# Every product of a two-layer encoder in plain float32 instead of three float32r products

## The chip, the cores and the metric

One core of a Trainium2 chip runs the whole program. The metric is device time of one execution in microseconds, the median of several runs. TensorE (PE in the profile) does the matrix products, VectorE (DVE) and ScalarE (ACT) the elementwise work, and the SyncE queue (SP) issues all transfers.

## What is computed

A trunk of two layers over 1024 tokens of width 1024. All inputs are float32. Cut to what matters:

```python
for layer in range(2):
    hn = rmsnorm(h, norm1_g[layer])
    proj = hn @ w_in[layer]                      # 1024 x 3328: u, q, k, v, gate_a, gate_b
    y_a = s5_branch(u, ...)                      # state-space branch, two directions, then GLU (512 x 512)
    y_b = windowed_gqa(q, k, v, sink, bias)      # 8 query heads of 64, 2 key heads, window 128
    merged = gate_a * (y_a @ w_branch_a[layer]) + gate_b * (y_b @ w_branch_b[layer])
    h = h + merged @ w_out[layer]
    hn2 = rmsnorm(h, norm2_g[layer])
    ff = silu(hn2 @ ffn_w_gate[layer]) * (hn2 @ ffn_w_up[layer])     # width 2816
    h = h + ff @ ffn_w_down[layer]
return rmsnorm(h, final_g)
```

## The kernel before, in words

Activations lie with channels on the 128 partitions and tokens along the free axis, in tiles of 128 x 512 (two token halves, `h` = 0 and 1). A dense layer is a loop over output tiles; for each, `chain` runs over the tiles of the contraction and adds into one 128 x 512 PSUM tile. A weight "granule" is 128 x 1024 floats, eight weight tiles that serve one output tile (or two) for both token halves, so 16 products.

**Two parts for every operand.** Each operand of a dense product is kept as a pair: `hi` is the value rounded to float32r (a ScalarE copy), `lo` is the rest (a VectorE subtraction). `split` (lines 87 to 91) does it for activations, `parts` (97 to 105) for weights, and `chain` (107 to 118) forms every product as three matmuls:

```python
mm(ps, lhsT=wh, rhs=xh, start=k == 0, stop=False)          # line 116
mm(ps, lhsT=wh, rhs=xl, start=False, stop=False)           # line 117
mm(ps, lhsT=wl, rhs=xh, start=False, stop=k == n - 1)      # line 118
```

The names in the trace: `pj` input projections, `glu`, `br` the two branch products, `wo` the output projection, `fg`, `fu`, `dn` the feed-forward's gate, up and down products.

**Attention.** A head has 64 channels, half of the partitions. For the scores (`att_scores`, line 716, tile `s`) the query tile holds hi of a head on one half of the partitions and lo on the other; the key tile holds the same keys on both halves, once as hi and once as lo, so that two matmuls over all 128 partitions give the whole product. For p times v (`att_values`, line 756, tile `pv`) the value tile holds hi and lo in two column halves; the sum of both halves is made on ScalarE and VectorE (lines 758 and 768). The probabilities are turned with transposes on TensorE (line 744, tile `pt`).

**The state-space branch** was in plain float32 all along: `s5x` (line 865, outputs on alternate halves of 64 PSUM partitions), `s5y` (lines 907 to 910), `psE` (lines 565 and 569, outputs on four quarters), and also the bias table `psb` (line 196, one 512-column product).

**What sets the order.** The program is a list of items (`build`), mixed by hand so that state-space and softmax work on VectorE lies beside dense products; `emit` runs through it. Weights are loaded on the SP queue into two `raw` buffers (`fetch`), then split into one of three hi/lo pairs, `LOOK` = 2 granules ahead. TensorE, VectorE and ScalarE run their items in the order of the list in the first part of layer 0 (`self.strict`).

Of the kernel before, what the change touches and what calls it, by code (L numbers as in the profile page):

```python
# [9 lines left out]
F32R = mybir.dt.float32r  # L10
# [29 lines left out]
LOOK = 2  # L40
# [3 lines left out]
W_BUFS = 3  # L44
# [4 lines left out]
class Granule:  # L49


    def __init__(self, src, n, slots=False):
        self.src, self.n, self.slots = src, n, slots
        self.raw = self.hi = self.lo = None
# [18 lines left out]
class Trunk:  # L73
# [13 lines left out]
    def split(self, src, name):  # L87
        hi, lo = self.A(name + "h", F32R), self.A(name + "l", F32R)
        self.nc.scalar.copy(hi, src)
        self.nc.vector.tensor_tensor(lo, src, hi.bitcast(F32), SUB)  # L90
        return hi, lo

    def fetch(self, g):
        g.raw = self.pw.tile([P, DM], F32, tag="raw", name="raw", bufs=2)
        self.nc.sync.dma_start(g.raw[:, :g.n], g.src)

    def parts(self, g):
        nc, n = self.nc, g.n
        if g.slots:
            g.hi, g.lo = self.A("whs", F32R), self.A("wls", F32R)  # L100
        else:
            g.hi = self.pw.tile([P, DM], F32R, tag="whi", name="whi", bufs=W_BUFS)
            g.lo = self.pw.tile([P, DM], F32R, tag="wlo", name="wlo", bufs=W_BUFS)
# [19 lines left out]
    def emit(self):  # L123
# [8 lines left out]
        self.order, self.fetched, self.split_ = order, 0, 0  # L132
        pos = {id(g): i for i, g in enumerate(order)}
        strict = None
        for i, (fn, gs) in enumerate(self.seq):
# [7 lines left out]
            if gs:  # L143
                self.ahead(max(pos[id(g)] for g in gs) + 1)
                held = [g.src.tensor.name for g in order[:self.split_] if last[id(g)] >= i and not g.slots]
                assert len(held) <= W_BUFS, (i, held)
            fn()
            if gs:
                n = max(pos[id(g)] for g in gs) + 1
                while self.split_ < len(order) and self.split_ < n + (7 if order[self.split_].slots else LOOK):  # L150
                    held = sum(last[id(g)] > i and not g.slots for g in order[:self.split_])
                    if held >= W_BUFS and not order[self.split_].slots:
                        break
                    self.ahead(self.split_ + 1)
                    if order[self.split_ - 1].slots:
                        break
# [5 lines left out]

    def ahead(self, n):
        n = min(n, len(self.order))
        while self.split_ < n:
            self.fetch_to(min(self.split_ + 2, len(self.order)))
            self.parts(self.order[self.split_])
            self.split_ += 1
# [86 lines left out]
    def normed(self, x, h, gi, name, out):  # L255

        nc = self.nc
        ys = {}
        for m in range(KT + 1):
            if m < KT:  # L260
                ys[m] = self.A("y")
                nc.vector.scalar_tensor_tensor(ys[m], x(m), self.gains[:, gi, m:m + 1], self.r[h], MUL, MUL)
            if m:
                out[m - 1] = self.split(ys.pop(m - 1), name)
            if m in (2, 4, 6):
                yield
# [10 lines left out]
    def first_pair(self, h, m, x):  # L277

        nc, g = self.nc, self.gains[:, 0, m:m + 1]
        hi, lo = self.A("xgh", F32R), self.A("xgl", F32R)  # L280
        nc.scalar.activation(hi, x, AF.Copy, scale=g)
        nc.vector.scalar_tensor_tensor(lo, x, g, hi.bitcast(F32), MUL, SUB)
        self.xg[h][m] = (hi, lo)
# [344 lines left out]
    def key_tiles(self, kn, kv, T):  # L628

        nc = self.nc  # L630
        s = slice(64 * kv, 64 * kv + 64)
        hh, ll = self.A(f"kh{kv}{T}", F32R), self.A(f"kl{kv}{T}", F32R)
        for o in (slice(0, 64), slice(64, 128)):
            nc.scalar.copy(hh[o], kn[T][s])
        for o in (slice(0, 64), slice(64, 128)):
            nc.vector.tensor_tensor(ll[o], kn[T][s], hh[s].bitcast(F32), SUB)
        self.kt[kv, T] = (hh, ll)

    def value_tiles(self, vn):
        nc = self.nc  # L640
        for T in range(2):
# [3 lines left out]
            for b in range(2):  # L645
                vt = self.A("vt", F32R)
                o = vt.rearrange("p (k s d) -> p k s d", s=2, d=64)
                src = pt[:, b * 256:(b + 1) * 256].rearrange("p (k d) -> p k d", d=64)
                nc.scalar.copy(o[:, :, 0], src)
                nc.vector.tensor_tensor(o[:, :, 1], src, o[:, :, 0].bitcast(F32), SUB)  # L650
                self.vt.append(vt)

    def tile_q(self, l, i, xs=None):
        nc = self.nc
        st = {}

        def done(h, ps):
# [6 lines left out]
            lo, up = slice(0, 64), slice(64, 128)  # L664
            for T in range(2):
                e, o = self.A(f"qe{i}{T}", F32R), self.A(f"qo{i}{T}", F32R)
                nc.scalar.copy(e[lo], qn[T][lo])
                nc.vector.tensor_tensor(e[up], qn[T][lo], e[lo].bitcast(F32), SUB)
                nc.scalar.copy(o[up], qn[T][up])
                nc.vector.tensor_tensor(o[lo], qn[T][up], o[up].bitcast(F32), SUB)  # L670
                self.qt[2 * i, T], self.qt[2 * i + 1, T] = e, o
# [22 lines left out]
    def att_scores(self, l, kv, b):  # L694
# [8 lines left out]
        for h in range(4):  # L703
            hd = 4 * kv + h
            q = self.qt[hd, Tq][:, (3 - oq) * P:(4 - oq) * P]
            ps = self.PS("s")
            spans = []
            a = k0
            while a < k1:
                e = min(k1, (a // 4 + 1) * 4)  # L710
                spans.append((a, e))
                a = e
            for w in range(2):
                for a, e in spans:
                    kk = self.kt[kv, a // 4][w]
                    nc.tensor.matmul(ps[:, (a - k0) * P:(e - k0) * P], lhsT=q, rhs=kk[:, (a % 4) * P:(a % 4 + e - a) * P],
                                     start=w == 0 and a == k0, stop=w == 1 and e == k1)
            x = self.A("x")
            V.tensor_tensor_reduce(out=x[:, :n], in0=ps[:, :n], in1=self.bias[hd][:, bo:bo + n], op0=ADD, op1=ALU.min,  # L719
                                   scale=-1.0, scalar=self.nsink[:, l, hd:hd + 1], accum_out=nm[:, h:h + 1])  # L720
            ex.append(x)
# [16 lines left out]
    def att_transpose(self, ex, k0, k1):  # L738
        nc = self.nc
        out = []  # L740
        for k in range(k1 - k0):
# [3 lines left out]
            out.append(self.split(ps, "p"))  # L745
        return out

    def att_values(self, kv, b, pt, k0, k1):
# [3 lines left out]
        for k in range(n):  # L752
            vb = k0 + k
            v = self.vt[vb // 2][:, (vb % 2 * 2 + kv) * P:(vb % 2 * 2 + kv + 1) * P]
            for w in range(2):
# [7 lines left out]
        w = slice((3 - o) * P, (4 - o) * P)  # L763
        for h in range(4):
            y = self.yb[2 * kv + h // 2, T]
            hp = slice(64 * (h % 2), 64 * (h % 2) + 64)
            c = slice(h * P, (h + 1) * P)
            nc.vector.tensor_tensor(y[hp, w], ps[0:64, c], t[0:64, c], ADD)

    def att_pairs(self, kv):  # L770

        nc = self.nc
        for i in range(2):
            kt = 2 * kv + i
            for h in range(2):
                hi, lo = self.A(f"ybh{kt}", F32R), self.A(f"ybl{kt}", F32R)
                for T in range(2):
                    s = self.yb[kt, T][:, ::-1].rearrange("p (n j) -> p j n", j=8)[:, 4 * h:4 * h + 4]
                    w = slice(64 * T, 64 * T + 64)
                    ho = hi.rearrange("p (j n) -> p j n", j=4)[:, :, w]  # L780
                    lw = lo.rearrange("p (j n) -> p j n", j=4)[:, :, w]
                    nc.scalar.copy(ho, s)
                    nc.vector.tensor_tensor(lw, s, ho.bitcast(F32), SUB)
                self.ybp[h][kt] = (hi, lo)
# [225 lines left out]
    def glu_items(self, l):  # L1010
        nc, V = self.nc, self.nc.vector
        gs = [self.pair_weights("w_glu", l, i) for i in range(2)]
        z, zp = {}, [[None] * 4, [None] * 4]
# [8 lines left out]
        def pairs(k):  # L1022
            for h in range(2):
                zp[h][k] = self.split(z[k, h], f"zp{k}")

        def run(h, m):
            ps = self.PS("glu")
            self.chain(ps, gs[m // 2], (m % 2) * HC, zp[h])
            t = self.A("gt")
# [145 lines left out]
    def build(self):  # L1175
# [14 lines left out]
        def start():  # L1190
# [9 lines left out]
            for h in range(2):  # L1200
                self.ahead(h + 1)
                for m in range(KT):
                    self.first_pair(h, m, xs[h][m])
# [232 lines left out]
```

## Time and profile before

| | before |
|---|---|
| median of 3 runs | 2757.1 us (2756.61 to 2757.65) |
| the profiled execution's own time | 2755.04 us |
| its span, first to last instruction | 2753.3 us |
| TensorE matmul busy | 2687.4 us, 13122 records |
| VectorE busy | 1548.3 us, 3321 records |
| ScalarE busy | 877.1 us, 1637 records |
| mean granted TensorE clock | 0.988 of full |

How to read it: a matmul's record runs from its start to the end of its results, so neighbours overlap. What a matmul costs in a dense stretch is the distance from one start to the next (or a stretch divided by its number of records), not the record's length. A float32r matmul has one record. A plain float32 matmul of the program has two records of equal form: the loop around line 907 runs 64 times (2 layers, 8 calls, 2 x 2 inside) and the trace has 128 records of it.

### The profile page before, as it was taken

The page shows a single profiled execution, that of the slowest core. Times are in us where ns is not written, and L with a number is a line of the kernel's source. Part 1 is how long each engine was busy: PE and PEld are TensorE (multiplying, and loading weights), DVE is VectorE, ACT ScalarE, POOL GpSimd, SP SyncE. Part 2 cuts the span into 40 slices and gives each one's busy share as a digit, 9 for nine tenths or more (in the row PEclk, how much of TensorE's full clock was granted, in tenths as well). Part 3 has the DMA queues.
Part 4 walks back from the last instruction along what each step waited for, and adds up shares of the span by engine and source line. Part 5 has one row for each costly group of instructions (what it writes and reads, how often), then busy time and mean ns, then how long its engine had stood idle before and what let it go on. Part 6 is the DMA issues. An engine that isn't in the chain of part 4 may idle for free.

```text
span 2753.3 us, 33872 instructions
## 1 busy us (share of the span) xinstructions
PE 2687.4 (98%) x13122; PEld 2226.9 (81%) x13122; DVE 1548.3 (56%) x3321; ACT 877.1 (32%) x1637; POOL 0.2 (0%) x4
## 2 busy tenths in 40 slices
PE   8999988999999999999999999999999999999997
PEld 6788876787888888888888888888878888888886
DVE  9987978675744444553376877565362323232335
ACT  5336744422312222221245643353131111111112
POOL 0000000000000000000000000000000000000000
PEclk9999998999999999999999999999999999999999
DMA  3453245342122221322221236444211111111111
GB/s 118 136 182 101 90 156 163 121 167 96 44 72 68 61 77 58 94 60 90 62 92 66 66 110 200 154 142 136 90 58 34 59 45 55 39 61 35 58 50 65
DMA packets 135920, 249.91 MB, mean 91 GB/s; under 512 B 14624, under 2 KB 50720, under 8 KB 135760
## 3 DMA queue, kind: packets, MB, share of 16 engines
q1 hardware_dynamic: 135760, 247.76, 27.9%
q8 instruction: 103, 1.69, 0.3%
q14 instruction: 57, 0.47, 0.1%
HBM read 187.98 MB, written 59.72 MB: 90 GB/s over the span
## 4 chain that ended last, share of the span: by engine, by line
PE 87%; DVE 8%; ACT 2%; DMA 1%; issue 1%; SPq 1%; DVEq 0%; ACTq 0%
PE fu L116 6%; PE fu L118 6%; PE fu L117 6%; PE dn L116 6%; PE fg L116 6%; PE fg L118 6%; PE dn L118 6%; PE dn L117 6%; PE fg L117 6%; PE pj L116 6%; PE pj L117 5%; PE pj L118 5%; PE wo L116 2%; PE wo L118 2%; PE wo L117 2%; PE br L117 2%
## 5 line engine op out<-in xcount | busy, mean ns | idle before, releaser
L104 ACT CAST whi<-raw 128x1024 fp32r<-128x1024 f32 (+2 forms) x240 | 228.3, 952 | 840.4 <-PE dn L117 315.5
L105 DVE TENSOR_TENSOR wlo<-raw,whi 128x1024 fp32r<-128x1024 f32 (+2 forms) x240 | 263.6, 1098 | 284.3 <-ACT whi L104 276.0
L116 PE MATMUL pj<-rah,whi 128*128 128x512 f32 x768 | 307.6, 402 | 6.8 <-DVE sm L719 6.8
L117 PE MATMUL pj<-ral,whi 128*128 128x512 f32 x768 | 302.0, 393 | 0.1
L118 PE MATMUL pj<-rah,wlo 128*128 128x512 f32 x768 | 301.7, 393 | 0.0
L117 PE MATMUL fg<-rfl,whi 128*128 128x512 f32 x704 | 274.8, 390 | 2.1 <-DVE rfl L90 2.1
L116 PE MATMUL fg<-rfh,whi 128*128 128x512 f32 x704 | 274.7, 390 | 0.0
L116 PE MATMUL fu<-rfh,whi 128*128 128x512 f32 x704 | 274.6, 390 | 0.0
L118 PE MATMUL fg<-rfh,wlo 128*128 128x512 f32 x704 | 274.0, 389 | 0.0
L117 PE MATMUL fu<-rfl,whi 128*128 128x512 f32 x704 | 274.0, 389 | 0.0
L118 PE MATMUL fu<-rfh,wlo 128*128 128x512 f32 x704 | 273.9, 389 | 0.0
L1124 DVE TENSOR_TENSOR h<-h,dn 128x512 f32<-128x512 f32 x160 | 109.7, 686 | 232.8 <-PE dn L118 232.4
L1116 DVE SCALAR_TENSOR_TENSOR ts<-fu,ts 128x512 f32<-128x512 f32 x88 | 60.8, 691 | 231.7 <-PE fu L118 231.7
L116 PEld LDWEIGHTS pj<-rah,whi 128*128 128x128 f32 x768 | 145.9, 190 | 41.3 <-DVE sm L719 8.0
L118 PEld LDWEIGHTS pj<-rah,wlo 128*128 128x128 f32 x768 | 145.5, 189 | 31.5
L117 PEld LDWEIGHTS pj<-ral,whi 128*128 128x128 f32 x768 | 145.9, 190 | 29.8 <-DVE ral L90 1.2
L117 PEld LDWEIGHTS fg<-rfl,whi 128*128 128x128 f32 x704 | 132.2, 188 | 32.6 <-DVE rfl L90 5.6
L118 PEld LDWEIGHTS fu<-rfh,wlo 128*128 128x128 f32 x704 | 132.2, 188 | 27.4
L117 PEld LDWEIGHTS fu<-rfl,whi 128*128 128x128 f32 x704 | 132.2, 188 | 27.3
L116 PEld LDWEIGHTS fg<-rfh,whi 128*128 128x128 f32 x704 | 132.2, 188 | 27.3
L116 PEld LDWEIGHTS fu<-rfh,whi 128*128 128x128 f32 x704 | 132.2, 188 | 27.2
L118 PEld LDWEIGHTS fg<-rfh,wlo 128*128 128x128 f32 x704 | 132.2, 188 | 27.2
(363 smaller groups left out, 4953.5 us busy)
## 6 DMA issues: line engine op xcount, KB each, us to landing
raw<-in_w_in SPq DMA_DIRECT2D x52, 512.0 KB
raw<-in_w_gate SPq DMA_DIRECT2D x44, 512.0 KB
raw<-in_w_up SPq DMA_DIRECT2D x44, 512.0 KB
g<-th SPq DMA_DIRECT2D x64, 256.0 KB
thr<-g SPq DMA_DIRECT2D x64, 256.0 KB
raw<-in_w_down SPq DMA_DIRECT2D x48, 256.0 KB
raw<-in_w_down SPq DMA_DIRECT2D x32, 320.0 KB
sp<-CA SPq DMA_DIRECT2D x64, 128.0 KB
```

The lines of the kernel that those rows point to most:

```text
L104: nc.scalar.copy(g.hi[:, :n], g.raw[:, :n])
L105: nc.vector.tensor_tensor(g.lo[:, :n], g.raw[:, :n], g.hi[:, :n].bitcast(F32), SUB)
L116: mm(ps, lhsT=wh, rhs=xh, start=k == 0, stop=False)
L117: mm(ps, lhsT=wh, rhs=xl, start=False, stop=False)
L118: mm(ps, lhsT=wl, rhs=xh, start=False, stop=k == n - 1)
L1116: V.scalar_tensor_tensor(s, st[h, "u"], 0.5, s, MUL, MUL)
L1124: V.tensor_tensor(x, x, ps, ADD)
```

## The change

All pairs go. Activations are single float32 tiles; weights are loaded straight into one of eight buffers (`W_BUFS` = 8, `LOOK` = 5 granules ahead) and used from there, so nothing on ScalarE or VectorE stands between the load and the product, and TensorE itself sets a weight buffer free. `chain` issues one plain float32 matmul where it issued three. Scores: keys of one head group stand twice, on both partition halves; a query tile holds two heads, one per half, and each head's product contracts over its own 64 partitions, two heads in turn, into two PSUM tiles. p times v: two heads' results go to PSUM partitions 0 to 63 and two to 64 to 127, 256 columns each, so the adding of halves after it goes too. A few factors of 0.25 and 0.5 move into other operations.

```diff
-LOOK = 2
+LOOK = 5
-W_BUFS = 3
+W_BUFS = 8
...
     def fetch(self, g):
-        g.raw = self.pw.tile([P, DM], F32, tag="raw", name="raw", bufs=2)
-        self.nc.sync.dma_start(g.raw[:, :g.n], g.src)
-
-    def parts(self, g):
...
-        nc.scalar.copy(g.hi[:, :n], g.raw[:, :n])
-        nc.vector.tensor_tensor(g.lo[:, :n], g.raw[:, :n], g.hi[:, :n].bitcast(F32), SUB)
+        g.w = self.A("ws") if g.slots else self.pw.tile([P, DM], F32, tag="w", name="w", bufs=W_BUFS)
+        self.nc.sync.dma_start(g.w[:, :g.n], g.src)
...
-        for k, (xh, xl) in enumerate(xs):
+        for k, x in enumerate(xs):
             if part is not None and k * 2 // n != part:
                 continue
             s = off + k * P
-            wh, wl = g.hi[:, s:s + P], g.lo[:, s:s + P]
-            mm = self.nc.tensor.matmul
-            mm(ps, lhsT=wh, rhs=xh, start=k == 0, stop=False)
-            mm(ps, lhsT=wh, rhs=xl, start=False, stop=False)
-            mm(ps, lhsT=wl, rhs=xh, start=False, stop=k == n - 1)
+            self.nc.tensor.matmul(ps, lhsT=g.w[:, s:s + P], rhs=x, start=k == 0, stop=k == n - 1)
...
+        for i in range(2):
+
+            pss = [self.PS("s") for _ in range(2)]
+            q = self.qt[2 * kv + i, Tq]
+            for a, e in spans:
+                for j, ps in enumerate(pss):
+                    r = slice(64 * j, 64 * j + 64)
+                    nc.tensor.matmul(ps[:, (a - k0) * P:(e - k0) * P], lhsT=q[r, (3 - oq) * P:(4 - oq) * P],
+                                     rhs=self.kt[kv, a // 4][r, (a % 4) * P:(a % 4 + e - a) * P], start=a == k0, stop=e == k1)
...
-            v = self.vt[vb // 2][:, (vb % 2 * 2 + kv) * P:(vb % 2 * 2 + kv + 1) * P]
-            for w in range(2):
-                nc.tensor.matmul(ps, lhsT=v, rhs=pt[k][w], start=k == 0 and w == 0, stop=k == n - 1 and w == 1)
-        t = self.A("pvl")
-        nc.scalar.copy(t[0:64], ps[64:128])
+            v = self.vt[vb // 4][:, vb % 4 * P + 64 * kv:vb % 4 * P + 64 * kv + 64]
+            p = pt[k].rearrange("p (i j q) -> p j i q", i=2, j=2)
+            for j in range(2):
+
+                nc.tensor.matmul(ps[64 * j:64 * j + 64, 0:256].rearrange("p (i q) -> p i q", i=2), lhsT=v, rhs=p[:, j],
+                                 start=k == 0, stop=k == n - 1)
...
-        for h in range(4):
-            y = self.yb[2 * kv + h // 2, T]
-            hp = slice(64 * (h % 2), 64 * (h % 2) + 64)
-            c = slice(h * P, (h + 1) * P)
-            nc.vector.tensor_tensor(y[hp, w], ps[0:64, c], t[0:64, c], ADD)
+        for i in range(2):
+            nc.vector.tensor_copy(self.yb[2 * kv + i, T][:, (3 - o) * P:(4 - o) * P], ps[:, i * P:(i + 1) * P])
```

How the instructions stand, at two places. First TensorE at the first down products of layer 0 (`fu` the last up product, `dn` down, `ts` the activation that was split into `ff..h` and `ff..l`). Before:

```order
L118 MATMUL fu<-rfh,wlo 128x512
L116 MATMUL dn<-ff0h,whi 128x512
L117 MATMUL dn<-ff0l,whi 128x512
L118 MATMUL dn<-ff0h,wlo 128x512
L116 MATMUL dn<-ff1h,whi 128x512
L117 MATMUL dn<-ff1l,whi 128x512
L118 MATMUL dn<-ff1h,wlo 128x512
```

Now, from the feed-forward's first products on:

```order
L97 MATMUL fg<-rf,w 128x512 x16
L97 MATMUL fu<-rf,w 128x512 x8
L97 MATMUL fg<-rf,w 128x512 x8
L97 MATMUL fu<-rf,w 128x512 x16
L97 MATMUL fg<-rf,w 128x512 x16
L97 MATMUL fu<-rf,w 128x512 x16
```

One instruction stands where three stood, with the same columns; the order of the products is as it was. Over the program 10560 such instructions become 3520.

Second, TensorE at one step of attention in layer 0 (`qe`, `qo` the query tiles with hi and lo, `kh`, `kl` the keys; now `qn` holds two heads and `kk` the keys). Before:

```order
L716 MATMUL s<-kh_2177,qe_714 128x384
L716 MATMUL s<-kl_2178,qe_714 128x384
L716 MATMUL s<-kh_2177,qo_715 128x384
L716 MATMUL s<-kl_2178,qo_715 128x384
L716 MATMUL s<-kh_2177,qe_832 128x384
L716 MATMUL s<-kl_2178,qe_832 128x384
L716 MATMUL s<-kh_2177,qo_833 128x384
L716 MATMUL s<-kl_2178,qo_833 128x384
L744 MATMUL pt<-cst,x 128x128 x8
```

Now (with the p times v of the step that follows):

```order
L658 MATMUL s<-kk_1513,qn_501 128x384 x2
L658 MATMUL s<-kk_1513,qn_537 128x384 x2
L689 MATMUL pt<-cst,x 128x128 x8
L97 MATMUL pj_1820<-ra,w 128x512 x8
L658 MATMUL s<-kk_1513,qn_501 128x384 x2
L658 MATMUL s<-kk_1513,qn_537 128x384 x2
L704 MATMUL pv<-p,vt 64x256 x4
```

Eight float32r instructions for a step's scores become four plain ones, in pairs of two heads on the two partition halves; p times v keeps its number of instructions (176 in the program), each of half the columns and half the output partitions.

## Rows read from the trace of the kernel before

**Rows 1.** The page: busy time by engine, and TensorE's busy tenths in 40 slices
```profile
PE 2687.4 (98%) x13122; PEld 2226.9 (81%) x13122; DVE 1548.3 (56%) x3321; ACT 877.1 (32%) x1637; POOL 0.2 (0%) x4
...
PE   8999988999999999999999999999999999999997
```

**Rows 2.** The page: the chain that ended last, by engine
```profile
PE 87%; DVE 8%; ACT 2%; DMA 1%; issue 1%; SPq 1%; DVEq 0%; ACTq 0%
```

**Rows 3.** Waits of PE, longest first: us in total, times, longest
```profile
PE s5x L865 <- DMA s5uk<-ud: 14.5, 4, 5.9
PE pj L116 <- ACT xgh L281: 7.1, 1, 7.1
...
PE br L116 <- ACT ybh L782: 3.8, 1, 3.8
```

**Rows 4.** Stretches of 100 us: busy us and (records) of each engine, clock, DMA
```profile
2100.00:2200.00 100.00, 100.00 (x443) 82.84 (x442) 30.03 (x41) 14.91 (x21) 0.00 (x0) 1.00 0.17 52
2500.00:2600.00 100.00, 100.00 (x443) 82.80 (x442) 32.73 (x46) 16.55 (x24) 0.00 (x0) 1.00 0.14 42
```

**Rows 5.** The same view over the whole span, line 116 alone
```profile
0.00:2754.00 2754.00, 1388.88 (x3520) 666.22 (x3520) 0.99 0.28 91
```

**Rows 6.** Line 196: durations min/median/max ns, first and last start; then the timeline
```profile
L196 PE MATMUL psb<-oh,rb x2: 584/584/585, 109.9 to 110.4; 32*8 32x512 f32 x2
...
109.92 1.01 PE L196 MATMUL psb<-oh,rb 32*8 32x512 f32 x2 [1.87 <-DMA rb<-in_rel_bias]
```

**Rows 7.** Timeline of PE: start us, us; first and last of 12 `s5y` products
```profile
404.49 0.38 PE L907 MATMUL s5y<-s5uk 128*128 128x128 f32 x2
...
406.94 0.39 PE L910 MATMUL s5y<-s5sg,s5ca 128*128 128x127 f32 x2
```

**Rows 8.** The chain in order of time: one step of scores, one of p times v
```profile
278.65 1.41 PE s L716 x8
280.06 1.39 PE pv L756 x6
```

**Rows 9.** Timeline of PE: 16 records of `s5x`, on alternate halves of the output partitions
```profile
358.19 1.10 PE L865 MATMUL s5x<-s5uk,s5wbt 128*64 128x128 f32 x16
```

**Rows 10.** The page: the splits of the weights on ACT and DVE
```profile
L104 ACT CAST whi<-raw 128x1024 fp32r<-128x1024 f32 (+2 forms) x240 | 228.3, 952 | 840.4 <-PE dn L117 315.5
L105 DVE TENSOR_TENSOR wlo<-raw,whi 128x1024 fp32r<-128x1024 f32 (+2 forms) x240 | 263.6, 1098 | 284.3 <-ACT whi L104 276.0
```

**Rows 11.** The chain in order of time: a weight load, and PE's last piece
```profile
15.11 4.29 DMA raw<-in_w_in
...
2742.08 2.09 PE psn L249 x8
```

**Rows 12.** Span and mean granted clock
```profile
core 0: 2753.3 us, clock 0.988
```

**Rows 13.** Timeline of PE after a wait of 3 us: longer records, then normal ones
```profile
454.27 1.97 PE L865 MATMUL s5x<-s5uk,s5wbt 128*64 128x128 f32 x16 [3.01 <-DMA s5uk<-ud]
...
456.77 0.63 PE L117 MATMUL br<-ybl,whi 128*128 128x512 f32 x1
457.19 0.63 PE L118 MATMUL br<-ybh,wlo 128*128 128x512 f32 x1
...
460.43 0.40 PE L117 MATMUL br<-ybl,whi 128*128 128x512 f32 x1
460.66 0.40 PE L118 MATMUL br<-ybh,wlo 128*128 128x512 f32 x1
```

**Rows 14.** Timeline of PE: six microseconds of plain float32 work, and what follows
```profile
481.89 0.38 PE L907 MATMUL s5y<-s5uk 128*128 128x128 f32 x2
...
486.84 1.10 PE L865 MATMUL s5x<-s5uk,s5wbt 128*64 128x128 f32 x16 [1.08 <-DMA s5uk<-ud]
...
488.21 0.40 PE L117 MATMUL br<-ybl,whi 128*128 128x512 f32 x1
488.45 0.40 PE L118 MATMUL br<-ybh,wlo 128*128 128x512 f32 x1
```

More of the change, by code (lines that the diff above doesn't have):

```diff
@@ L9 @@
 F32 = mybir.dt.float32
-F32R = mybir.dt.float32r
 I32 = mybir.dt.int32
@@ L53, in __init__ @@
         self.src, self.n, self.slots = src, n, slots
-        self.raw = self.hi = self.lo = None
+        self.w = None
 class Later:
@@ L143, in emit @@
             if gs:
-                self.ahead(max(pos[id(g)] for g in gs) + 1)
-                held = [g.src.tensor.name for g in order[:self.split_] if last[id(g)] >= i and not g.slots]
-                assert len(held) <= W_BUFS, (i, held)
+                n = max(pos[id(g)] for g in gs) + 1
+                self.fetch_to(n)
+                held = [g for g in order[:self.fetched] if last[id(g)] >= i and not g.slots]
+                assert len(held) <= W_BUFS, (i, len(held))
             fn()
             if gs:
[L149 to L152, printed above, removed]
+                while self.fetched < len(order) and self.fetched < n + LOOK:
+                    g = order[self.fetched]
+                    if not g.slots and sum(last[id(x)] > i and not x.slots for x in order[:self.fetched]) >= W_BUFS:
                         break
-                    self.ahead(self.split_ + 1)
-                    if order[self.split_ - 1].slots:
+                    self.fetch_to(self.fetched + 1)
+                    if g.slots:
                         break
@@ L161, in fetch_to @@
             self.fetched += 1
[L163 to L168, printed above, removed]
     def constants(self):
@@ L255, in normed @@
     def normed(self, x, h, gi, name, out):
[L257 to L265, printed above, removed]
+        for m in range(KT):
+            out[m] = self.A(name)
+            self.nc.vector.scalar_tensor_tensor(out[m], x(m), self.gains[:, gi, m:m + 1], self.r[h], MUL, MUL)
+            if m in (1, 3, 5):
                 yield
@@ L275, in first_half, with first_gain @@
         return xs
[L277 to L283, printed above, removed]
+    def first_gain(self, h, m, x):
+        self.xg[h][m] = self.A("xg")
+        self.nc.scalar.activation(self.xg[h][m], x, AF.Copy, scale=self.gains[:, 0, m:m + 1])
     def s5_scalars(self):
@@ L628, in key_tiles @@
     def key_tiles(self, kn, kv, T):
-        nc = self.nc
-        s = slice(64 * kv, 64 * kv + 64)
-        hh, ll = self.A(f"kh{kv}{T}", F32R), self.A(f"kl{kv}{T}", F32R)
+        kk = self.kt[kv, T] = self.A(f"kk{kv}{T}")
         for o in (slice(0, 64), slice(64, 128)):
[L634 to L637, printed above, removed]
+            self.nc.scalar.copy(kk[o], kn[T][64 * kv:64 * kv + 64])
     def value_tiles(self, vn):
@@ L644, in value_tiles @@
                 nc.tensor.transpose(pt[:, b * P:(b + 1) * P], vn[T][:, b * P:(b + 1) * P], self.ident)
[L645 to L651, printed above, removed]
+            self.vt.append(self.A("vt"))
+            nc.scalar.copy(self.vt[T], pt)
     def tile_q(self, l, i, xs=None):
-        nc = self.nc
         st = {}
@@ L702, in att_scores @@
         ex = []
-        for h in range(4):
[L704 to L712, printed above, removed]
-            for w in range(2):
[L714 to L721, printed above, removed]
+        spans = [(a, min(k1, (a // 4 + 1) * 4)) for a in range(k0, k1) if a == k0 or a % 4 == 0]
+        for i in range(2):
[6 more added lines that the diff above has]
+                                     rhs=self.kt[kv, a // 4][r, (a % 4) * P:(a % 4 + e - a) * P], start=a == k0, stop=e == k1)
+            for j, ps in enumerate(pss):
+                h = 2 * i + j
+                hd = 4 * kv + h
+                x = self.A("x")
+                V.tensor_tensor_reduce(out=x[:, :n], in0=ps[:, :n], in1=self.bias[hd][:, bo:bo + n], op0=ADD, op1=ALU.min,
+                                       scale=-1.0, scalar=self.nsink[:, l, hd:hd + 1], accum_out=nm[:, h:h + 1])
+                ex.append(x)
         for h in range(4):
@@ L744, in att_transpose @@
                 nc.tensor.transpose(ps[:, h * P:(h + 1) * P], ex[h][:, k * P:(k + 1) * P], self.ident)
-            out.append(self.split(ps, "p"))
+            out.append(self.A("p"))
+            nc.scalar.copy(out[k], ps)
         return out
@@ L775, in att_pairs @@
             for h in range(2):
-                hi, lo = self.A(f"ybh{kt}", F32R), self.A(f"ybl{kt}", F32R)
+                y = self.ybp[h][kt] = self.A(f"yp{kt}")
                 for T in range(2):
                     s = self.yb[kt, T][:, ::-1].rearrange("p (n j) -> p j n", j=8)[:, 4 * h:4 * h + 4]
[L779 to L784, printed above, removed]
+                    nc.scalar.copy(y.rearrange("p (j n) -> p j n", j=4)[:, :, 64 * T:64 * T + 64], s)
     def bias_load(self, kv):
@@ L1020, in prep @@
                 nc.sync.dma_start(z[k, h].rearrange("p (j n) -> p j n", j=4), self.zd[k][:, 4 * h:4 * h + 4, :])
-        def pairs(k):
-            for h in range(2):
-                zp[h][k] = self.split(z[k, h], f"zp{k}")
         def run(h, m):
             ps = self.PS("glu")
-            self.chain(ps, gs[m // 2], (m % 2) * HC, zp[h])
-            t = self.A("gt")
+            self.chain(ps, gs[m // 2], (m % 2) * HC, [z[k, h] for k in range(4)])
+            t = self.ya[h][m] = self.A(f"ya{m}")
             nc.scalar.activation(t, ps, AF.Tanh, scale=0.25)
             V.scalar_tensor_tensor(t, t, 1.0, z[m, h], ADD, MUL)
-            hi, lo = self.A(f"yah{m}", F32R), self.A(f"yal{m}", F32R)
-            nc.scalar.activation(hi, t, AF.Copy, scale=0.25)
-            V.scalar_tensor_tensor(lo, t, 0.25, hi.bitcast(F32), MUL, SUB)
-            self.ya[h][m] = (hi, lo)
         for h in range(2):
@@ L1039, in glu_items @@
                 out.append((lambda h=h, m=m: run(h, m), gs[m // 2]))
-        early = [(lambda k=k: prep(k),) for k in range(4)]
-        split = [(lambda k=k: pairs(k),) for k in range(4)]
-        return early, split, out
+        return [(lambda k=k: prep(k),) for k in range(4)], out
     def w_out_items(self, l):
@@ L1116, in up_out @@
             V.scalar_tensor_tensor(s, st[h, "u"], 0.5, s, MUL, MUL)
-            ff[h][f] = self.split(s, f"ff{f % 6}")
+            ff[h][f] = s
         def down(gi, m, h, g):
@@ L1200, in start @@
             for h in range(2):
-                self.ahead(h + 1)
                 for m in range(KT):
-                    self.first_pair(h, m, xs[h][m])
+                    self.first_gain(h, m, xs[h][m])
         self.item(start)
@@ L1274, in done_a @@
                 V.scalar_tensor_tensor(t, t, 1.0, ps, ADD, MUL)
-                V.tensor_tensor(t, t, b, ADD)
-                hi, lo = self.A(f"mgh{m}", F32R), self.A(f"mgl{m}", F32R)
-                nc.scalar.activation(hi, t, AF.Copy, scale=0.5)
-                V.scalar_tensor_tensor(lo, t, 0.5, hi.bitcast(F32), MUL, SUB)
-                self.mg[h][m] = (hi, lo)
+                mg = self.mg[h][m] = self.A(f"mg{m}")
+                V.tensor_tensor(mg, t, b, ADD)
             bb = self.branch_items(l, "w_br_b", lambda h: self.ybp[h], (), done_b)
             ba = self.branch_items(l, "w_br_a", lambda h: self.ya[h], (ta, tb), done_a)
-            early, split, glu = self.glu_items(l)
+            early, glu = self.glu_items(l)
             if l == 0:
@@ L1288, in build @@
             n = min(4, len(left))
-            self.add(early[:3] + split[:3] + left[:n // 2] + early[3:] + (pairs[:1] if l else []) + left[n // 2:n] + split[3:] +
+            self.add(early[:3] + left[:n // 2] + early[3:] + (pairs[:1] if l else []) + left[n // 2:n] +
                      (self.mix(glu, pairs[1:]) if l else glu))
```

30 lines of the change are left out of this document (5 added, 25 removed).

## The prediction, made before the changed kernel was run

> **What bounds the kernel now.** I read the page first, then the waits, then TensorE's timeline. The busy line [rows 1] has TensorE at 2687.4 us of a span of 2753.3, VectorE at 1548.3 and ScalarE at 877.1; the slices show TensorE at 9 tenths nearly everywhere. The chain that ended last is TensorE for 87% [rows 2]. The waits [rows 3] are short: the longest class is 14.5 us in all. So the kernel's time is the time of TensorE's instruction stream, and the question is what one product costs as three float32r matmuls, and what as one plain matmul.
>
> Busy time can't answer that, because records overlap. Two stretches of the feed-forward that hold nothing but chains have 443 records in 100 us each, at a granted clock of 1.00 [rows 4]: 100 / 443 = 0.2257 us from start to start. Three of them are **0.677 us per product**. Line 116 has 3520 records [rows 5], one per product, so chains take 3520 x 0.677 = 2383 us of the span.
>
> **What a plain product costs.** The kernel already runs some, each seen as two records. The only one with 512 columns is the bias table's [rows 6]: two records of 0.584 us, 1.01 us together, so the second starts 1.01 - 0.584 = 0.43 us after the first. That is nearly twice the 0.2257 us of a float32r record of the same columns, and there are two of them. The `s5y` products have 128 columns [rows 7]: from the first start to the twelfth, 2.45 us, so 2.45 / 11 = 0.2227 us per product, 0.1114 per record. Both fit two periods of the full 2.4 GHz clock per column (0.833 ns, so 0.427 us at 512 columns and 0.1067 at 128) plus about 5 ns a record. I take 2 x (0.4267 + 0.0047) = **0.863 us per product**. The lower bound is 0.853, with nothing between records; the upper one 4 x 0.2227 = 0.891, if what lies between records grows with the columns. I take the value near the lower end because the 512-column row is the nearest in form, and its 0.43 has no room for the upper one.
>
> The Trainium skill, "FP8 and Floating Point Precision", section "TensorE Precision Notes", says that a true FP32 product takes four passes through the array. Four passes at the float32r record's 0.2257 us would be 0.903 us per product and the sum below some 140 us higher; the trace shows two records per product, each about twice as long, and 0.43 us each is 0.86.
>
> **The change part by part.** All counts are of the whole program.
>
> 1. *Chains.* 3520 x (0.863 - 0.677) = **+655 us**, all of it on the path, since nothing else is longer than TensorE. By the bounds +619 and +753.
>
> 2. *Scores.* A step with three key blocks took 1.41 us for eight matmuls [rows 8]; 24 of 32 steps have that width, the other 8 two thirds of it: 24 x 1.41 + 8 x 0.95 = 41 us. Now four plain products of 384 columns, two records each of 384 x 0.833 + 5 = 325 ns: 2.60 us in a row, or 1.30 if the two partition halves run side by side. For column halves the trace shows that they do: 16 records of `s5x`, 128 columns, take 1.10 us with the last one's 0.27 [rows 9], so 0.83 / 15 = 0.055 us each, half of the 0.1114 that a lone one costs. No row has two row halves. I take side by side: 24 x 1.30 + 8 x 0.87 = 38 us, **-3 us**; the other end is +35.
>
> 3. *p times v.* 88 key blocks at 1.39 / 3 = 0.463 us [rows 8] are 41 us. Now each block has two column halves of 256 columns, two records each: 4 x 218 ns, halved by running side by side as `s5x` does: 0.436 us, 38 us, **-3 us**. One after the other it would be +36.
>
> 4. *Splits.* The weights' splits alone, 228.3 us on ScalarE and 263.6 on VectorE [rows 10], and those of activations and probabilities go. They lay beside TensorE's work and were not what it waited for, so they are worth nothing by themselves. The transposes, the state-space products and the softmax stay.
>
> 5. *Weights straight from the load.* A granule now feeds 16 x 0.863 = 13.8 us of work (10.8 before), and a load was seen to land 4.29 us after issue even in the crowded start [rows 11]. With five granules ahead I cost it at nothing. The new wait is that a load needs TensorE to be done with the buffer, and what is behind it on the SP queue (state-space loads and stores) waits too. Eight buffers and five ahead mean that the buffer asked for was left some three granules, 40 us, earlier, so I expect no queueing; if that cover is gone, the state-space loads come late and the 14.5 us of rows 3 would perhaps double, +15.
>
> 6. *Idle time and slow stretches.* TensorE is idle 2753.3 - 2687.4 = 66 us. The first 7.1 us are the load of the first operands [rows 3], and after its last piece, at 2742.08 + 2.09, come 9 us of final scaling [rows 11]; both stay. Of the other 50 (state-space loads, softmax, the split of `ybh`) I take half away: each dense item between two such steps is now 27% longer, and ScalarE and VectorE have less ahead of them. **-25 us**. The mean granted clock is 0.988 [rows 12], that is 33 us of full-speed work not done, a part of it in the idle ends. After a wait of 3 us the records run at the lower level, 1.2 GHz, for some 6 us [rows 13]: starts 0.42 us apart, and 0.23 after it. Fewer waits mean fewer such stretches: **-10 us**. Bounds for both together: 0 and -75.
>
> Sum: 2753.3 + 655 - 3 - 3 - 25 - 10 = 3367 us of span. The median of the runs is 3.8 us above the profiled span, so **3371 us**, 22% slower.
>
> **The rivals.**
>
> *The price between records is higher* (chance 0.12). At 0.891 per product, part 1 is +753 and the time 3469; at four float32r passes, 0.903, it is +796 and 3512. For it: no row shows a long run of 512-column plain products. Against it: the 0.43 us of rows 6.
>
> *The halves don't run side by side* (0.07). Scores alone: 3371 + 38 = 3409; p times v too: 3448. For it: no row with row halves, and two heads are issued in turn, each with two records. Against it: rows 9, for column halves.
>
> *The two records of a product lie over each other, or one of them is spared* (0.04): this ends on the other side. One record for a product costs 0.431 us instead of 0.677, the chains 1519 us instead of 2383, and the kernel some 2757 - 864 - 6 = 1887 us, with TensorE still the longest engine after the splits are gone. The mechanism would be that the 128-column products are paced by the loading of their weights, so that their 0.1114 us says nothing of the columns, and that the bias product, with 8 output columns, is a case apart. It decides from a price below 0.677 + 0.012 = 0.689 us per product, where the sum of the parts crosses zero. Against it: rows 6 have both a load of 8 weight columns and 0.43 us from record to record. The Trainium skill, "Perfetto Trace Analysis", section "Engine Utilization", gives the array half its output rate for FP32_LOW_HIGH; read as a price of a whole product, that would be this rival. Each record here does run at half the rate, but there are two.
>
> *Plain work does not hold the full clock* (0.02). At 1.2 GHz throughout, 3520 products would cost 1.73 us each and the kernel over 6400 us. Against it: 6 us of nothing but plain work with one 1.08 us wait in it [rows 14], after which float32r starts are 0.24 us apart, the pace of the full clock.
>
> **How the numbers follow.** My forecast has 0.74. Its own range: chains at 0.853 with most idle time gone give 3371 - 36 - 40 = 3295, at 0.875 with none gone 3371 + 42 + 35 = 3448; I don't expect both ends at once. The range of 8 in 10, 3320 to 3480, holds most of the forecast, the rival of the halves whole and the lower end of the rival of the price (3469). Left out are 3512, the fast rival and the slow clock. Slower by over 0.2% (what a measurement of this kernel can tell from no change): 0.74 + 0.12 + 0.07 + 0.02 = 0.95. Faster: 0.04. The remaining 0.01 is for prices that happen to meet at the crossing.
>
> **What would show it.** In the changed kernel's profile, a stretch of 100 us in the feed-forward should hold 100 / 0.4314 = 232 matmul records, 116 products, at clock 1.00. 215 to 225 records mean the higher price; 443 would mean that a plain record costs what a float32r one did. The records of line 97 should number 7040. A step of scores should take about 1.3 us from its first start to the next work, 2.6 if the halves run one after the other; a step of p times v 1.3 against 2.6. TensorE should be busy 98 to 99% of the span, VectorE well under half. The prediction is wrong if the feed-forward's pace is not 0.43 us a record, or if TensorE waits for weights.

## The result, and the profile after

The changed kernel takes 3336.98 us (median of 4 runs, 3335.31 to 3337.30) against 2757.38 us before (2756.61 to 2759.78): ratio 1.2099, 95% interval 1.2078 to 1.2120. It is 21% slower; 3371 us within 3320 to 3480 was forecast. The profiled execution took 3337.3 us with a span of 3335.5, so the span grew by 582.2 us.

The page of the changed kernel, as in [rows 1, 2]: busy time, TensorE's slices, its granted clock, and the chain that ended last.

```profile
PE 3294.5 (99%) x9778; PEld 1538.9 (46%) x9778; DVE 1019.8 (31%) x2593; ACT 483.5 (14%) x1097; POOL 0.2 (0%) x4
...
PE   8999998999999999999999999999999999999998
...
PEclk9999999999999999999999999999999999999999
...
PE 97%; DVE 2%; DMA 1%; ACT 0%; SPq 0%; issue 0%; DVEq 0%; ACTq 0%
```

TensorE was the bound before and is it more purely now: its share of the chain rose from 87 to 97%, while VectorE lost 528 us of work and ScalarE 394. None of that work comes back as time. TensorE's busy time grew by 607.1 us and its idle time fell from 65.9 to 41.1, which makes the 582.2.

The dense products of the changed kernel: the costliest group on TensorE, then all records of line 97 over the span and a stretch of the feed-forward as in [rows 4, 5].

```profile
L97 PE MATMUL pj<-ra,w 128*128 128x512 f32 x1536 | 673.2, 594 | 0.0
```

```profile
0.00:3336.00 3336.00, 3055.37 (x7040) 1332.54 (x7040) 0.99 0.24 75
```

```profile
2500.00:2600.00 100.00, 100.00 (x235) 44.29 (x234) 13.79 (x20) 2.13 (x4) 0.00 (x0) 1.00 0.13 40
```

Each of the 3520 products has two records, 7040. The exact pace is in the chain in order of time, where a long run without any wait stands as one piece (start, us, what):

```profile
2547.78 68.67 PE dn L97 x160
```

68.67 / 160 = 0.4292 us per record, **0.8584 us per product**. The same measure before, from the timeline, with 45 records from the first start to the second:

```profile
1400.11 0.39 PE L118 MATMUL dn<-ff0h,wls 128*128 128x512 f32 x1
...
1410.33 0.39 PE L118 MATMUL dn<-ff3h,wls 128*128 128x512 f32 x1
```

10.22 / 45 = 0.2271 us, **0.6813 us per product** of three. The difference of 0.1771 us, 3520 times, is 623 us.

TensorE's waits, longest first, as in [rows 3], and the mean clock, as in [rows 12]:

```profile
PE s5x L803 <- DMA s5uk<-ud: 11.3, 5, 4.1
PE pj L97 <- ACT xg L247: 8.3, 1, 8.3
PE glu L97 <- DMA z<-zd: 4.5, 1, 4.5
```

```profile
core 0: 3335.5 us, clock 0.995
```

The waits for the softmax are gone from the list, those for state-space loads and for the first operands stay, and no wait for weights appears.

To see where TensorE's time went I charged each record with the time until the next record's start (its own length if a gap follows), over both whole traces:

| us of TensorE | before | after |
|---|---|---|
| dense products | 2437.4 | 3042.2 |
| scores | 44.8 | 44.4 |
| p times v | 41.1 | 42.6 |
| transposes, state space, norms, bias | 164.1 | 165.2 |
| idle | 65.9 | 41.1 |

The dense products are +605 us: 623 from the pace, and -18 because 39 us above the pace before became 21 (less time at the slower clock after waits, and no longer some 0.09 us more for the first float32r matmul after transposes and other whole-array work).

### The profile page after: what moved, and what is told of

It reads as the page before. It is cut to its first block, busy times and chain, and to the rows that moved or that the text cites. A ratio compares the mean times of both kernels' runs of the same rounds, so it can differ in the third digit from the quotient of the medians.

```text
span 3335.5 us, 25628 instructions
## 1 busy us (share of the span) xinstructions
PE 3294.5 (99%) x9778; PEld 1538.9 (46%) x9778; DVE 1019.8 (31%) x2593; ACT 483.5 (14%) x1097; POOL 0.2 (0%) x4
## 4 chain that ended last, share of the span: by engine, by line
PE 97%; DVE 2%; DMA 1%; ACT 0%; SPq 0%; issue 0%; DVEq 0%; ACTq 0%
PE pj L97 21%; PE dn L97 18%; PE fg L97 18%; PE fu L97 18%; PE wo L97 7%; PE br L97 6%; PE glu L97 2%; PE s L658 1%; PE pt L689 1%; PE pv L704 1%; PE s5x L803 1%; PE pswb L513 0%; PE psn L221 0%; DVE s5z L821 0%; PE s5y L848 0%; PE s5y L845 0%
## 5 line engine op out<-in xcount | busy, mean ns | idle before, releaser
L97 PE MATMUL pj<-ra,w 128*128 128x512 f32 x1536 | 673.2, 594 | 0.0
L97 PE MATMUL fg<-rf,w 128*128 128x512 f32 x1408 | 613.0, 592 | 0.0
L97 PE MATMUL fu<-rf,w 128*128 128x512 f32 x1408 | 612.4, 592 | 0.0
L97 PE MATMUL dn<-ts,w 128*128 128x512 f32 x1152 | 496.7, 592 | 0.0
L97 PEld LDWEIGHTS pj<-ra,w 128*128 128x128 f32 x1536 | 286.7, 190 | 340.5 <-issue 336.6
L97 PEld LDWEIGHTS fu<-rf,w 128*128 128x128 f32 x1408 | 267.3, 190 | 334.2 <-issue 334.0
L97 PEld LDWEIGHTS fg<-rf,w 128*128 128x128 f32 x1408 | 267.0, 190 | 332.3 <-issue 330.9
L97 PEld LDWEIGHTS dn<-ts,w 128*128 128x128 f32 x1152 | 218.6, 190 | 273.1 <-issue 272.5
L97 PE MATMUL wo<-mg,w 128*128 128x512 f32 x512 | 220.9, 593 | 0.0
L97 PE MATMUL br<-yp,w 128*128 128x512 f32 x256 | 119.7, 612 | 1.9 <-ACT yp L722 1.9
```

The lines of the kernel that those rows point to most:

```text
L97: self.nc.tensor.matmul(ps, lhsT=g.w[:, s:s + P], rhs=x, start=k == 0, stop=k == n - 1)
```

## The experiments

The ratios compare each kernel with the kernel before on the same chip, whose median was 2753 to 2754 us in these sets of runs and 2757 in that of the changed kernel. So the times alone do not tell an experiment from the changed kernel when they differ by a few microseconds; there the traces, charged as above, have to decide.

### Only the dense products

After's program with attention as before (float32r parts, splits of q, k, v and p):

```diff
-            out.append(self.A("p"))
-            nc.scalar.copy(out[k], ps)
+            out.append(self.split(ps, "p"))
...
+            for w in range(2):
+                for a, e in spans:
+                    kk = self.kt[kv, a // 4][w]
```

> Only the dense products are plain; attention keeps its float32r parts and their splits. My theory: the dense products carry the whole change. The changed kernel's TensorE has 44.4 us of scores and 42.6 of p times v against 44.8 and 41.1 before, so this version should take 3337 us within 10, perhaps up to 3350 if the splits of the probabilities delay the softmax. Rival: the change of attention hides a gain (fewer splits, fewer waits) that the dense products' loss covers; then this version is some 25 us slower than the changed kernel, 3362 us.

Measured: 3335.8 us (3333.9 to 3338.4), ratio 1.2117 (1.2101 to 1.2134), not to be told from the whole change. The dense products carry the loss. Once they are plain, attention's change takes 7.5 us of TensorE's busy time (3287.0 without it, 3294.5 with it) and gives back 4 us of its idle time, which the times don't tell from nothing.

### Only attention

Before's program with attention as after, dense products in three parts:

```diff
-            out.append(self.split(ps, "p"))
+            out.append(self.A("p"))
+            nc.scalar.copy(out[k], ps)
...
-            for w in range(2):
-                for a, e in spans:
-                    kk = self.kt[kv, a // 4][w]
+            for a, e in spans:
+                for j, ps in enumerate(pss):
+                    r = slice(64 * j, 64 * j + 64)
```

> Only attention is changed (plain float32 on halves, no splits of q, k, v, p); the dense products keep three float32r matmuls. My theory: on TensorE nothing changes (86 us of scores and p times v either way), and VectorE, 85% busy between 200 and 400 us, has about 150 us less to do; where TensorE waited for it (10 us for sm) a few us go: 2740 to 2757 us. Rival: the switching between whole array and halves costs on every step, 64 times in and out at 0.1 us or more: 2757 to 2775 us.

Measured: 2738.7 us (2737.9 to 2740.8), ratio 0.9948 (0.9935 to 0.9962): **faster than both kernels**, by 0.5% against the kernel before, and just below the range that I had expected. Charged as above, its scores and p times v own 44.4 and 42.6 us of TensorE, as in the changed kernel. What shrank is VectorE's work and TensorE's waiting. The stretch from 200 to 400 us, attention of layer 0, before and with attention alone changed (busy us and records of PE, PEld, DVE, ACT, POOL; clock, DMA share, GB/s):

```profile
200.00:400.00 200.00, 193.54 (x1142) 164.04 (x1141) 170.64 (x511) 123.40 (x308) 0.00 (x0) 0.98 0.33 109
```

```profile
200.00:400.00 200.00, 196.39 (x1237) 148.76 (x1223) 125.75 (x426) 110.20 (x288) 0.00 (x0) 1.00 0.36 119
```

VectorE goes from 85 to 63% busy, and TensorE, which waited for it before, idles 3.6 us instead of 6.5 there; over the span TensorE's idle time is 2737.2 - 2683.8 = 53 us instead of 66. The waits of the kernel before that end with the softmax's `sm` on VectorE are these:

```profile
PE pj L116 <- DVE sm L719: 6.8, 5, 1.9
...
PE pt L744 <- DVE sm L719: 3.4, 2, 2.0
```

With attention alone changed, 1.0 us of these 10.2 is left. So in attention VectorE was late, and its work there was not free. Which part of that work it was is not shown: the splits of q, k, v and p went together with the adding of halves after p times v. Those of q and k are not needed for it, since they are back in the last experiment and the wait for `sm` stays at 1.0 us. The rival, a price of switching, is not the larger effect.

### Dense products plain, but all splits kept

```diff
-            mm = self.nc.tensor.matmul
-            mm(ps, lhsT=wh, rhs=xh, start=k == 0, stop=False)
-            mm(ps, lhsT=wh, rhs=xl, start=False, stop=False)
-            mm(ps, lhsT=wl, rhs=xh, start=False, stop=k == n - 1)
+            self.nc.tensor.matmul(ps, lhsT=wh, rhs=xh, start=k == 0, stop=k == n - 1)
...
-            g.hi = self.pw.tile([P, DM], F32R, tag="whi", name="whi", bufs=W_BUFS)
+            g.hi = self.pw.tile([P, DM], F32, tag="whi", name="whi", bufs=W_BUFS)
```

> Dense products plain as in the changed kernel, but every split of the dense operands on ScalarE and VectorE is kept as work whose low part nobody uses (the high part is an exact copy), with the old loads and look-ahead; attention as before. My theory: splits are hidden by TensorE in either form, and TensorE's waits shrank because the items between them got longer: the time equals that of the version with only the dense products changed, within 10 us. Rival: the 25 us of idle time that went from TensorE went because the splits went; then this version is 20 to 30 us slower than that one.

Measured: 3337.1 us (3336.0 to 3339.2), ratio 1.2122 (1.2106 to 1.2139), against 3335.8 without the splits. The page of this kernel:

```profile
PE 3289.9 (99%) x9602; PEld 1569.7 (47%) x9602; DVE 1560.6 (47%) x3321; ACT 876.0 (26%) x1637; POOL 0.2 (0%) x4
```

```profile
```

VectorE has 430 us and ScalarE 350 us more to do than with only the dense products changed (1131.0 and 525.5), and the time is the same within 1.3 us. TensorE idles 47 us, as it does there (45), though the splits are all back (TensorE waits for their high parts alone). So 18 of the 25 us that its idle time fell came with the plain products, not with the end of the splits. That the longer dense items between the waits are the reason is the reading left; no run tries it by itself.

### Dense products in pieces of 256 columns

```diff
-            self.nc.tensor.matmul(ps, lhsT=g.w[:, s:s + P], rhs=x, start=k == 0, stop=k == n - 1)
+            for c in (slice(0, 256), slice(256, 512)):
+                self.nc.tensor.matmul(ps[:, c], lhsT=g.w[:, s:s + P], rhs=x[:, c], start=k == 0 and c.start == 0, stop=k == n - 1 and c.start > 0)
```

> The changed kernel with every dense product issued as two of 256 columns: 14080 records instead of 7040, the same columns. A record of 512 columns starts 0.4292 us after the one before, 2.5 ns above 512 x 0.8333. If the 2.5 ns are a fixed price of a record, a product costs 4 x (213.3 + 2.5) = 863 ns instead of 858 and the kernel 17 us more, 3354 us. If what lies between records grows with the columns, it stays at 3337. If short records are paced by something else, as the 128-column ones with their 4.7 ns above the columns suggest (for example the loading of weights, one per record), 872 ns and 3385 us or more.

Measured: 3354.2 us (3350.3 to 3358.2), 17 us more, as the fixed price has it; the dense products own 14 us more in the trace. The chain in order of time, the same down products as above in twice as many records:

```profile
2555.80 69.07 PE dn L98 x320
```

69.07 / 320 = 0.2158 us, which is 256 x 0.8333 + 2.5 ns. A plain record costs its columns at two periods of 2.4 GHz each and 2.5 ns, at 256 and at 512 columns alike. The 4.7 ns that I took from the `s5y` products of 128 columns belong to those.

### The halves in another order: scores

```diff
-            for a, e in spans:
-                for j, ps in enumerate(pss):
-                    r = slice(64 * j, 64 * j + 64)
+        for j in range(2):
+            for i in range(2):
+                for a, e in spans:
+                    r = slice(64 * j, 64 * j + 64)
```

> The changed kernel, with a step's four score products issued in another order: the two of the lower partition half first, then the two of the upper, where the changed kernel alternates. If the two row halves run side by side in the changed kernel (my theory), neighbours on one half now run one after the other and only the middle pair overlaps: a step of 384 columns takes 3 x 0.65 us instead of 2 x 0.65, so 24 x 0.65 + 8 x 0.43 = 19 us more, 3356 us. Rival: the halves don't overlap, or overlap whatever the order; then no change, 3337 us.

Measured: 3341.8 us (3339.3 to 3343.0), ratio 1.2132 (1.2114 to 1.2150): 5 us more, not 19, in an interval that overlaps the changed kernel's. The trace shows it: charged as above, the scores own 50.7 us of TensorE instead of 44.4. The starts of the eight records of one step of 384 columns, in ns from the first:

```
changed kernel:     0    6  426  433  749  756 1071 1078
halves in order:    0   13  427  440  750  762 1071 1085
```

The side by side that the theory claims is plain in the first line: two records start 6 to 7 ns apart and the next pair 0.32 us later, which is 384 columns. But the second line, where both products of the lower half stand ahead of those of the upper, has pairs too. Only the steps whose keys lie in two tiles, with four instructions per half, got longer (timeline, the same step in the changed kernel and here):

```profile
298.13 1.58 PE L658 MATMUL s<-kk,qn 64*128 64x128 f32 x16
```

```profile
298.01 2.34 PE L656 MATMUL s<-kk,qn 64*128 64x128 f32 x16
```

So TensorE took records of the upper half ahead of up to four records of the lower half that stood before them. My size was wrong because I let it take them strictly in order.

### The halves in another order: p times v

```diff
-        for k in range(n):
...
-            for j in range(2):
+        for j in range(2):
+            for k in range(n):
```

> The changed kernel, with a step's p times v issued for all key blocks of one column half first, then for the other, where the changed kernel alternates. If column halves run side by side, a step of three blocks takes five times 0.43 us instead of three times, one of two blocks three times instead of two: 24 x 0.86 + 8 x 0.43 = 24 us more, 3361 us. Rival: no overlap in the changed kernel, 3337 us.

Measured: 3348.7 us (3346.1 to 3350.7), ratio 1.2158 (1.2137 to 1.2178): 12 us more, not 24. The step that starts at 299 us in the changed kernel and here:

```profile
299.65 1.52 PE L704 MATMUL pv<-p,vt 128*64 128x256 f32 x12
```

```profile
299.36 2.00 PE L703 MATMUL pv<-p,vt 128*64 128x256 f32 x12
```

0.48 us more a step, where the program's order, with only the middle pair side by side, would be 0.86. The first record of the second half starts 489 ns after the step's first, beside the third of six records of the first half; four of the six were then not done. The same reach of four as in the scores. Both runs show that the halves do run side by side: taking that away in part costs time.

### Shorter look-ahead

```diff
-LOOK = 5
+LOOK = 2
-W_BUFS = 8
+W_BUFS = 3
```

> The changed kernel with three weight buffers and two granules of look-ahead instead of eight and five. My theory (a granule feeds 13.8 us of work, a load needs 4 to 6 us): no change, 3337 us within 5. Rival: with three buffers the load of a granule waits on the SP queue for TensorE to leave the buffer, and state-space loads and stores wait behind it; the 11 us that TensorE waits for s5uk double or more, 3350 us and up.

Measured: 3340.3 us (3339.2 to 3340.8), ratio 1.2127 (1.2109 to 1.2145), 3 us above the changed kernel's median in an interval that overlaps its own. TensorE's wait for `s5uk` is 7.5 us here, not more than the 11.3 before. The deep look-ahead is worth no more than these few microseconds.

### Two float32r products instead of three

The kernel before without its line 118:

```diff
-            mm(ps, lhsT=wh, rhs=xl, start=False, stop=False)
-            mm(ps, lhsT=wl, rhs=xh, start=False, stop=k == n - 1)
+            mm(ps, lhsT=wh, rhs=xl, start=False, stop=k == n - 1)
```

> The kernel before without line 118: the product of the low part of the weights with the high part of the activations is left out, so each dense product is two float32r matmuls. If a float32r matmul costs 0.227 us of TensorE wherever it stands, 3520 x 0.227 = 799 us go: 1955 us. Rival: VectorE (1548 us busy) and the loads can't keep up with shorter products, and TensorE waits: 2000 to 2100 us.

Measured: 2166.2 us, ratio 0.7865 (0.7849 to 0.7881): the rival's kind of outcome, beyond its end. The page of this kernel:

```profile
PE 1963.9 (91%) x9602; PEld 1601.5 (74%) x9602; DVE 1535.1 (71%) x3321; ACT 874.5 (40%) x1637; POOL 0.2 (0%) x4
```

Dense stretches keep the pace (443 records from 1900 to 2000 us, as in [rows 4]), but TensorE idles 200 us instead of 66 and the mean granted clock falls to 0.945, so that the dense products own 1688 us, 89 above that pace (39 before). Of the waits in its list, 111 us end with VectorE, 40 with ScalarE and 37 with a DMA. The longest is for the squares of a norm:

```profile
PE psn L225 <- DVE sqb L216: 27.8, 4, 14.8
```

So at two thirds of the products' length VectorE's unchanged work is late in many places. Few of the waits end with a split itself (`wlo` 2.5 us, `pl` 4.7, `rfl` 4.6, `ral` 3.6); how much of the rest the splits cause by keeping VectorE busy is not shown, since no run has two products and no splits.

### Scores in float32r parts on halves

The version with attention alone changed, with the scores as three float32r products per head, two heads in turn:

```diff
-            for a, e in spans:
-                for j, ps in enumerate(pss):
+            for w, (wq, wk) in enumerate(((0, 0), (0, 1), (1, 0))):
+                for a, e in spans:
+                    for j, ps in enumerate(pss):
```

> As the version with attention alone changed (2739 us), but the scores keep three float32r products of parts, each head on its own partition half, two heads in turn. A float32r record of 384 columns was 0.173 us from its neighbour before. If float32r records of two halves run side by side as the plain ones do (my theory), a step of 384 columns takes 6 x 0.173 + 0.2 of switching = 1.24 us instead of 1.49, 24 x 0.25 + 8 x 0.17 = 7 us less on TensorE, and the splits of q and k that come back are hidden: 2731 us. Rival: they don't overlap; then a step takes 2.1 us, 19 us more: 2758 us.

Measured: 2737.3 us (2736.2 to 2739.6), ratio 0.9945 (0.9932 to 0.9959), not to be told from 2738.7: the 7 us expected did not come. A step in this kernel's timeline:

```profile
270.08 0.44 PE L704 MATMUL s<-kh,qh 64*128 64x384 f32 x2
...
271.33 1.51 PE L751 MATMUL pv<-p,vt 128*64 128x256 f32 x12
```

The step is 1.25 us long, as expected, so float32r halves run side by side as well, and the scores own 39.8 us of TensorE instead of 44.4. But TensorE's idle time rose from 53 to 56 us, so of the 3.1 us that its busy time fell most came back as waits.

## Why the prediction was right

Point by point, by the steps of the prediction.

**Step 1, the chains**, was the right mechanism and 32 us too large in pace: +655 for a measured +623. Half is the price of the plain product, 0.863 taken and 0.8584 measured: the 4.7 ns between records were carried over from 128 columns to 512, where it is 2.5 (shown with 256 columns). The other half is the old price: I divided 100 us by 443 records, but that view counts records that reach over both edges (235 now, where 100 / 0.4292 is 233), so 0.2257 should have been 0.2271 from start to start. The remaining 18 us below +623 are the slower stretches and the first float32r matmul after other work; of this I had forecast the clock's part in step 6. In the sum the 32 us of the pace are all that was off in the end: attention was forecast 7 us too fast and what the dense products take above the pace 9 us too slow, and that these nearly cancel is luck.

**Steps 2 and 3, attention**, came out at -0.4 and +1.5 us instead of -3 and -3. The halves run side by side, but entering and leaving a step costs: in the starts above the first pair of scores takes 0.426 us to the next instead of 0.32, and p times v follows 0.42 us after the last pair instead of 0.32. In p times v the first pair takes 0.27 us instead of 0.216, and the transposes follow 0.31 us after the last. In 32 steps each that is 6 us on the scores and 4 to 5 on p times v, which eats the gain. (Another 3 us stand with the dense products: the last of them before each step of scores takes 0.52 us instead of 0.429.) That the scores came out even is luck, for their old price was too low as well: eight of the steps with three key blocks have keys in two tiles and took 1.79 to 1.85 us before, where I had 1.41 for all, and take 1.51 now.

```profile
1508.85 1.85 PE s L716 x16
```


**Step 4, the splits at nothing**: shown with all splits kept, 3337.1 against 3335.8 us. It holds under plain products. Under float32r products attention's work on VectorE, of which splits are a part, was not free (attention alone, -0.5%).

**Step 5, weights straight from the load**: no cost, as forecast, but not for the reason I gave. The SP queue's own waits in the changed kernel say that it does stand before weight loads until TensorE leaves a buffer:

```profile
SPq L88 <- PE fg L97: 476.1, 40, 28.8
```

The queue runs ahead and waits, and what lies behind it is early enough even with three buffers.

**Step 6, idle time and clock**: idle 65.9 to 41.1 us, -25 as forecast. The mean granted clock rose from 0.988 to 0.995, so 33 us of full-speed work not done became 17, where I took 10 off.

The rivals: the higher price fell to 0.8584, below its lower end of 0.891. The trace has 7040 records of line 97, 0.4292 us apart, so no record is spared or lies over another. The halves run side by side, 6 to 7 ns apart. The clock was 1.00 in every stretch of 100 us from 600 to 3300 us. By the Trainium skill, "FP8 and Floating Point Precision", section "TensorE Precision Notes", a true FP32 product is four passes; by this count an estimate is four times 512 columns at 2.4 GHz, 0.853 us, and the run agrees with 0.8584. What was too high was to price each pass as a float32r record with all that lies between records.

## What to carry to other kernels

Read a matmul's price as the distance between starts in a run without waits, per record and per column; a plain float32 product of 512 columns was 0.858 us here against 0.227 for one float32r matmul, so three parts are cheaper than one plain product, and four would not be. Work that only prepares operands is free as long as the products beside it are long enough: the splits cost nothing that the runs could tell under plain products, while under float32r products VectorE's work in attention, splits included, cost 0.5%. With a third of the products taken away TensorE idled 200 us instead of 66, over half of its waits ending with VectorE. Changing only the part where the preparing engine is late (attention) gave the one kind of version that keeps every product and beats both kernels: 2739 us, and 2737 with the scores in float32r parts.

## What the runs showed of the hardware

- What lies between records depends on the kind: a plain float32 record of 256 or 512 columns costs 2.5 ns above its columns' time, a float32r record of 512 columns 0.2271 - 0.2133 us = 14 ns. Three float32r matmuls are 0.640 us of columns and 0.041 of the rest.
- Products on two halves of the array, by rows (plain and float32r) and by columns (plain), started within 15 ns of each other and ran at the pace of one. Records of the free half were taken ahead of up to four records of the busy half that stood before them in the program; with six ahead, the seventh started beside the third.
- Going from the whole array to row halves cost about 0.09 us at the last record before and 0.1 at the first after (0.52 and 0.43 us instead of 0.43 and 0.32), from row halves to column halves 0.09 and 0.05, and from column halves to the transposes 0.09 at the last record.
- The clock held its full level through 2.7 ms of nearly uninterrupted plain float32 products, with transposes and halves among them (granted clock 1.00 from 600 to 3300 us).
